# A causal convolution on one core: the middle outputs are finished by an accumulating DMA instead of VectorE

## The chip, the core and the metric

The kernel runs on one core of a Trainium2 chip. The core has five engines that matter here. TensorE (PE in the profile, with PEld for its weight loads) multiplies matrices into PSUM. VectorE (DVE) and ScalarE (ACT) do elementwise work on SBUF and PSUM. GpSimd (POOL) and SyncE (SP) issue DMAs here; POOL also makes a tiny copy now and then. Each engine runs its own list of instructions in the order in which it was written, and waits on semaphores where data of another engine or of a DMA is needed. The DMAs of all engines are carried by the same 16 DMA engines, those of SP through queue q1 and those of POOL through queue q0.

The metric is the device time of one execution in microseconds.

## The reference

```python
def reference(x, kernel):          # x: 8 x 4096 x 512, kernel: 8 x 512 x 512, f32
    out = np.zeros_like(x)
    for k in range(8):
        shifted = x if k == 0 else np.concatenate(
            [np.zeros((B, k, D)), x[:, :-k, :]], axis=1)
        out += np.matmul(shifted, kernel[k])
    return out
```

It is a causal convolution along the sequence with eight taps, and each tap is a 512 x 512 matrix. Output row t is the sum over k of x[t - k] times kernel[k].

## The kernel before

**Layout.** The 8 x 4096 rows of x are cut into 128 runs of 256 rows; run number is the partition. One "row" of the kernel is therefore 128 x 512 values, and a matmul takes 128 x 128 of it against a 128 x 512 piece of a weight. Four such matmuls are a *product* (`product`, L115 to L119): one row of 512 against one 512 x 512 matrix.

**Algorithm.** After four head rows that are computed directly, each block of 12 output rows is made with a nested Karatsuba-like scheme. The outer level splits a block into four *nodes*, PL, MI, H1 and H0, each of which is a smaller convolution of 4 output rows with combined inputs (sums and differences of rows, made on VectorE as Z, S, A and F) and combined weights. There are 21 blocks and so 84 nodes. For PL, MI and H1 a node has nine products of four matmuls, 36 matmuls; H0 is a leaf with eleven products, 44.

**What a node's result becomes.** Each node leaves two PSUM tiles, `p[LO]` and `p[HI]`, of two rows each. Step `e0` finishes the LO tile, step `e1` the HI tile (`node_e`, L225 to L244). With b for LO or HI:

- PL: ScalarE writes cc[b] = 0.5 PL (L229).
- MI: VectorE writes dd[b] = cc[b] - 0.5 MI, in a new tile (L232).
- H1: VectorE writes y = H1 + dd[b], stored as the first four rows of the block.
- H0: VectorE writes dd[b] = dd[b] - H0 in place, stored as the last four rows.
- `middle` (L246 to L249; steps `g0` for LO and `g1` for HI): VectorE writes cc[b] = 2 cc[b] - dd[b], which is half of PL + MI, and stores it as the middle four rows.

The tiles cc, dd and y come from one pool of five buffers (`y_tile`, L222). A tile is taken over when the last reader of the buffer's earlier tile is done, a DMA's landing included. All stores but one go through SP (`store`, L217).

**Order.** It is written out by hand. The first block is a long list of single steps (L506 to L594); from node 5 on the table SLOT gives each kind of node its steps:

```python
    SLOT = {
        PL: "s l00 F1 a0 l01 u l11 e0 s0 z s1 v0 F0 A x dt d0 v1 d1 l10 a1 e1",
        MI: "s l01 l00 F1 a0 u l11 e0 s0 z s1 dt A F0 v0 x v1 d1 l10 d0 e1 a1",
        H1: "s l00 F1 a0 l01 u l11 s0 dt e0 z s1 A F0 g0 v0 d0 r v1 d1 l10 e1",
        H0: "s l00 F1 b1 l01 a0 u e0 l11 s0 z s1 dt F0 A v0 x d0 g1 v1 d1 l10 a1 e1",
    }
```

Steps l00 to l11, a0, a1, b1, u, v0 and v1 are products on TensorE. Steps s, z, A, F0 and F1 make the inputs on VectorE, d0 and d1 are VectorE steps on PSUM. Steps s0, s1 and dt are ScalarE's: s0 and s1 (`node_seed`, L183) copy a partial result of the next node into its PSUM tiles, and the matmuls of v0 and later add to it. Much of a node's input work is done one or two nodes ahead: in step names "cur" is the node of the slot, s, s0, F0, v0, a0 and u belong to the next one, and z, A and a1 to the one after it.

**DMAs for the input.** Step `r` of H1 (`rows_ahead`) lets POOL make a small copy that waits for VectorE's A (`behind`, L106), and then issue three loads of x for a later block (L87; cast to bf16, into DRAM scratch xd). Step x lets SP issue the transposing DMAs from xd to the ring buffer XR (L94), two in PL and one in MI. So the order on POOL is: copy, three loads, and again in the next block. In blocks 19 to 21 nothing is left to load. In the first block the step r of H1 is written after g1 of H0, not before it.

Of the kernel before, what the change touches and what calls it, by code (L numbers as in the profile page):

```python
# [14 lines left out]
def kernel(  # L15
# [6 lines left out]
    nc = tc.nc  # L22
# [11 lines left out]
    ADD = mybir.AluOpType.add  # L34
    SUB = mybir.AluOpType.subtract
    MUL = mybir.AluOpType.mult
# [3 lines left out]
    orr = out.rearrange("b (g t) d -> (b g) t d", t=RUN)  # L40
# [39 lines left out]
    def tt(o, a, b, op):  # L80
        nc.vector.tensor_tensor(out=o, in0=a, in1=b, op=op)  # L81
# [135 lines left out]
    def store(t, y):  # L217
        nc.sync.dma_start(out=orr[:, t:t + 2, :], in_=y)

    cc, dd = {}, {}  # L220

    def y_tile():  # L222
        return ypool.tile([P, 2, D], f32, name="y")

    def node_e(n, b_):  # L225
        p, t = n.p[b_], n.t + 2 * b_
        if n.a == PL:
            cc[b_] = y_tile()
            nc.scalar.mul(out=cc[b_], in_=p, mul=0.5)  # L229
        elif n.a == MI:  # L230
            dd[b_] = y_tile()
            nc.vector.scalar_tensor_tensor(out=dd[b_], in0=p, scalar=-0.5,  # L232
                                           in1=cc[b_], op0=MUL, op1=ADD)
        elif n.a == H1:
            y = y_tile()
            tt(y, p, dd[b_], ADD)
            store(t, y)
        elif n.k == len(nodes) - 1 and b_ == HI:
            for j, eng in enumerate((nc.scalar, nc.sync)):
                tt(dd[b_][:, j], dd[b_][:, j], p[:, j], SUB)  # L240
                eng.dma_start(out=orr[:, t + 8 + j, :], in_=dd[b_][:, j])
        else:
            tt(dd[b_], dd[b_], p, SUB)
            store(t + 8, dd[b_])  # L244

    def middle(n, b_):  # L246
        nc.vector.scalar_tensor_tensor(out=cc[b_], in0=cc[b_], scalar=2.0,  # L247
                                       in1=dd[b_], op0=MUL, op1=SUB)
        store(n.t + 4 + 2 * b_, cc[b_])  # L249

    def load_w(tap):
        n = K - 1 - tap
# [85 lines left out]
    def step(k):  # L338
# [11 lines left out]
        def rows_ahead():  # L350
# [14 lines left out]
            "v0": (nxt, lambda: node_v(nxt, 0)), "v1": (nxt, lambda: node_v(nxt, 1)),  # L365
            "d0": (nxt, lambda: node_d(nxt, 0)), "d1": (nxt, lambda: node_d(nxt, 1)),
            "e0": (cur, lambda: node_e(cur, 0)), "e1": (cur, lambda: node_e(cur, 1)),
            "x": (cur, moves), "r": (cur, rows_ahead), "g0": (cur, lambda: middle(cur, 0)), "g1": (cur, lambda: middle(cur, 1)),
        }
        return acts  # L370
# [258 lines left out]
```

## Time and profile before

| | |
|---|---|
| median of 2 runs (lowest to highest) | 746.35 us (746.24 to 746.46) |
| span of the profiled execution, first to last instruction | 744.5 us |
| TensorE busy | 729.4 us, 98% |
| VectorE busy | 694.6 us, 93% |
| ScalarE busy | 241.3 us, 32% |
| POOL busy | 57.4 us, 8% |
| L247 on VectorE (the middle outputs) | 42 instructions, 51.1 us |
| L229 on ScalarE (0.5 PL) | 42 instructions, 43.1 us |
| q1 (SP) / q0 (POOL), share of the 16 DMA engines | 49.5% / 28.0% |
| read / written in HBM | 77.33 MB / 99.09 MB |
| granted TensorE clock | 1.00 |

In the page, the span goes from the first to the last instruction of the profiled execution; the runs' times also hold what lies around it, 1.9 us here. The median stands for runs without the details. A line such as "L87 POOL ... xd<-in_x_dram x3" means: code line 87, engine POOL, writes xd, reads in_x_dram, three instructions. In timelines the first column is the start and the second the duration, both in us. Busy shares are averages over the span and don't by themselves say which engine sets the end.

### The profile page before, as it was taken

Reading aid. Unit: us, or ns where it says so; the run is one execution under the profiler, and the core shown is the slowest. Engines: PE = TensorE matmul, PEld = TensorE weight load, DVE = VectorE, ACT = ScalarE, POOL = GpSimd, SP = SyncE. Lnnn points to the kernel's source line nnn. Section 1 sums busy time; section 2 is a strip of 40 time slices with the busy share of each in tenths; the row PEclk is TensorE's granted clock in tenths of the full one; section 3 lists DMA queues with packets and bytes.
Section 4 is the critical chain, followed back from the end, with each engine's and each line's share of the span. In section 5 each row is a group of like instructions: output and inputs, shape, how many; then the busy total and the mean of one; then the engine's idle time right before and its main releaser. Section 6 shows DMA issues by size and latency. Waiting matters only on the chain.

```text
span 744.5 us, 8887 instructions
## 1 busy us (share of the span) xinstructions
PE 729.4 (98%) x3362; PEld 331.6 (45%) x3430; DVE 694.6 (93%) x725; ACT 241.3 (32%) x368; POOL 57.4 (8%) x98
## 2 busy tenths in 40 slices
PE   8989999999999999999999999999999999999997
PEld 4434444444444444444444444444444444444443
DVE  1989999999999999999999999999999999999996
ACT  3053333332333333232323323242333323333331
POOL 4200010101010010101011010101101010100000
PEclk9999999999999999999999999999999999999999
DMA  9994979696886969697795969678595968865314
GB/s 202 210 208 134 227 152 246 138 237 160 199 208 160 247 136 241 148 219 185 183 233 136 246 141 234 170 178 238 138 242 137 248 156 189 220 148 194 124 78 170
DMA packets 159371, 138.88 MB, mean 187 GB/s; under 512 B 130144, under 2 KB 134240, under 8 KB 159200
## 3 DMA queue, kind: packets, MB, share of 16 engines
q1 hardware_dynamic: 145456, 99.89, 49.5%
q0 software_dynamic: 13728, 38.15, 28.0%
q8 instruction: 27, 0.44, 0.3%
q10 hardware_dynamic: 144, 0.26, 0.1%
q14 instruction: 16, 0.13, 0.0%
HBM read 77.33 MB, written 99.09 MB: 237 GB/s over the span
## 4 chain that ended last, share of the span: by engine, by line
PE 89%; DVE 4%; issue 1%; ACT 1%; DVEq 0%; ACTq 0%
PE pp L117 89%; DVE Z L81 1%; DVE y L81 1%; DVE S L81 0%; DVE w L81 0%; DVE y L247 0%; DVE A L81 0%; DVE pp L81 0%; DVE F L81 0%; ACT pp L187 0%; ACT pp L168 0%; ACT y L229 0%; ACT pp L189 0%; DVEq L624 0%; DVEq L81 0%
## 5 line engine op out<-in xcount | busy, mean ns | idle before, releaser
L117 PE MATMUL pp<-w,S 128*128 128x512 bf16 x1175 | 274.3, 379 | 1.3
L117 PE MATMUL pp<-w,F 128*128 128x512 bf16 x970 | 244.9, 379 | 1.1
L117 PEld LDWEIGHTS <-S 128*128 128x128 bf16 x1200 | 117.1, 98 | 142.9 <-issue 3.4
L117 PE MATMUL pp<-w,A 128*128 128x512 bf16 x661 | 170.6, 379 | 2.8 <-ACT pp L189 1.2
L81 DVE TENSOR_TENSOR Z<-XR 128x2048 bf16<-128x2048 bf16 (+3 forms) x109 | 154.2, 1432 | 0.1
L117 PEld LDWEIGHTS <-F 128*128 128x128 bf16 x992 | 97.0, 98 | 117.1
L81 DVE TENSOR_TENSOR S<-Z 128x2560 bf16<-128x2560 bf16 (+1 forms) x85 | 124.3, 1464 | 0.0
L187 ACT COPY pp<-pp 128x512 f32<-128x512 f32 (+1 forms) x84 | 57.8, 688 | 154.8 <-PE pp L117 152.0
L117 PEld LDWEIGHTS <-A 128*128 128x128 bf16 x672 | 65.2, 97 | 83.2 <-DVE A L81 4.4
L171 ACT COPY pp<-pp 128x512 f32<-128x512 f32 x62 | 35.3, 570 | 197.1 <-PE pp L117 197.1
L117 PE MATMUL pp<-w,Z 128*128 128x512 bf16 x330 | 85.4, 379 | 0.3
L81 DVE TENSOR_TENSOR F<-S 128x1024 bf16<-128x1024 bf16 x124 | 84.5, 682 | 0.0
L106 POOL COPY junk<-A 128x2 bf16<-128x2 bf16 x18 | 17.6, 977 | 557.6 <-DVE A L81 557.6
L189 ACT ACTIVATE pp<-pp 128x512 f32<-128x512 f32 (+1 forms) x84 | 58.6, 698 | 5.4 <-DVE y L232 2.8
L232 DVE SCALAR_TENSOR_TENSOR y<-pp,y 128x1024 f32<-128x1024 f32 x42 | 51.3, 1220 | 9.4 <-PE pp L117 9.0
L81 DVE TENSOR_TENSOR A<-Z 128x1024 bf16<-128x1024 bf16 x84 | 57.7, 686 | 1.4
L229 ACT ACTIVATE y<-pp 128x1024 f32<-128x1024 f32 x42 | 43.1, 1027 | 42.1 <-PE pp L117 40.1
L206 DVE SCALAR_TENSOR_TENSOR pp<-pp,DT 128x512 f32<-128x512 f32 x62 | 42.9, 692 | 14.3 <-PE pp L117 13.6
L81 DVE TENSOR_TENSOR y<-pp,y 128x1024 f32<-128x1024 f32 x42 | 51.1, 1216 | 1.8 <-DMA out_dram<-y 1.6
L81 DVE TENSOR_TENSOR y<-y,pp 128x1024 f32<-128x1024 f32 (+1 forms) x43 | 50.9, 1185 | 2.0 <-PE pp L117 2.0
L247 DVE SCALAR_TENSOR_TENSOR y<-y 128x1024 f32<-128x1024 f32 x42 | 51.1, 1216 | 0.0
L117 PEld LDWEIGHTS <-Z 128*128 128x128 bf16 x336 | 32.8, 98 | 39.7 <-DVE w L81 0.3
(28 smaller groups left out, 241.3 us busy)
## 6 DMA issues: line engine op xcount, KB each, us to landing
out_dram<-y SPq DMA_DIRECT2D x127, 512.0 KB, 7.5
xd<-in_x_dram POOLq DMA_DIRECT2D x61, 512.0 KB, 10.8
w<-in_kernel_dram POOLq DMA_DIRECT2D x8, 512.0 KB, 15.8
w<-in_x_dram SPq DMA_DIRECT2D x1, 1024.0 KB, 4.8
w<-in_x_dram POOLq DMA_DIRECT2D x2, 512.0 KB, 13.5
XR<-xd SPq DMA_TRANSPOSE x61, 5.0
w<-in_x_dram POOLq DMA_DIRECT2D x2, 256.0 KB, 18.5
w<-in_x_dram POOLq DMA_DIRECT2D x1, 384.0 KB, 20.1
```

The lines of the kernel that those rows point to most:

```text
L81: nc.vector.tensor_tensor(out=o, in0=a, in1=b, op=op)
L106: nc.gpsimd.tensor_copy(out=junk, in_=z[:, 0:2])
L117: nc.tensor.matmul(bank, lhsT=comp[:, c * P:(c + 1) * P], rhs=w[:, c, :], start=start and c == 0, stop=c == DC - 1, skip_group_check=True)
L171: nc.scalar.copy(out=n.q[:, 0], in_=n.q[:, 1])
L187: nc.scalar.copy(out=o, in_=q)
L189: nc.scalar.mul(out=o, in_=q, mul=-1.0)
L206: nc.vector.scalar_tensor_tensor(out=p[:, 0], in0=p[:, 1], scalar=-1.0, in1=DT, op0=MUL, op1=SUB)
L229: nc.scalar.mul(out=cc[b_], in_=p, mul=0.5)
L232: nc.vector.scalar_tensor_tensor(out=dd[b_], in0=p, scalar=-0.5, in1=cc[b_], op0=MUL, op1=ADD)
L247: nc.vector.scalar_tensor_tensor(out=cc[b_], in0=cc[b_], scalar=2.0, in1=dd[b_], op0=MUL, op1=SUB)
```

## The change

PL is now stored as it is: ScalarE copies it from PSUM to cc[b], which goes to the middle rows of the output at once, and ScalarE writes a second tile, dd[b] = -0.5 PL. MI adds half of itself to dd[b] in place, so dd[b] now holds the negative of what it held. H1 subtracts dd[b] instead of adding it; H0 writes -dd[b] - H0. `middle` is no longer a VectorE instruction and a store: POOL issues a DMA that adds dd[b] to the middle rows that are already in DRAM, so that PL becomes PL - 0.5 PL + 0.5 MI. Steps g0 and g1 keep their places in the written order.

```diff
         if n.a == PL:
             cc[b_] = y_tile()
-            nc.scalar.mul(out=cc[b_], in_=p, mul=0.5)
+            nc.scalar.copy(out=cc[b_], in_=p)
+            store(t + 4, cc[b_])
+            dd[b_] = y_tile()
+            nc.scalar.mul(out=dd[b_], in_=p, mul=-0.5)
         elif n.a == MI:
-            dd[b_] = y_tile()
-            nc.vector.scalar_tensor_tensor(out=dd[b_], in0=p, scalar=-0.5,
-                                           in1=cc[b_], op0=MUL, op1=ADD)
+            nc.vector.scalar_tensor_tensor(out=dd[b_], in0=p, scalar=0.5,
+                                           in1=dd[b_], op0=MUL, op1=ADD)
         elif n.a == H1:
             y = y_tile()
-            tt(y, p, dd[b_], ADD)
+            tt(y, p, dd[b_], SUB)
             store(t, y)
         elif n.k == len(nodes) - 1 and b_ == HI:
             for j, eng in enumerate((nc.scalar, nc.sync)):
-                tt(dd[b_][:, j], dd[b_][:, j], p[:, j], SUB)
+                nc.vector.scalar_tensor_tensor(out=dd[b_][:, j], in0=dd[b_][:, j], scalar=-1.0,
+                                               in1=p[:, j], op0=MUL, op1=SUB)
                 eng.dma_start(out=orr[:, t + 8 + j, :], in_=dd[b_][:, j])
         else:
-            tt(dd[b_], dd[b_], p, SUB)
+            nc.vector.scalar_tensor_tensor(out=dd[b_], in0=dd[b_], scalar=-1.0,
+                                           in1=p, op0=MUL, op1=SUB)
             store(t + 8, dd[b_])

     def middle(n, b_):
-        nc.vector.scalar_tensor_tensor(out=cc[b_], in0=cc[b_], scalar=2.0,
-                                       in1=dd[b_], op0=MUL, op1=SUB)
-        store(n.t + 4 + 2 * b_, cc[b_])
+        nc.gpsimd.dma_start(out=orr[:, n.t + 4 + 2 * b_:n.t + 6 + 2 * b_, :], in_=dd[b_], accum_op=ADD)
```

## The prediction

> **What bounds the kernel now.** I read the page's busy shares first, then the chain that ended last, then the group of the removed instruction.
>
> ```profile
> PE 729.4 (98%) x3362; PEld 331.6 (45%) x3430; DVE 694.6 (93%) x725; ACT 241.3 (32%) x368; POOL 57.4 (8%) x98
> PE 89%; DVE 4%; issue 1%; ACT 1%; DVEq 0%; ACTq 0%
> L247 DVE SCALAR_TENSOR_TENSOR y<-y 128x1024 f32<-128x1024 f32 x42 | 51.1, 1216 | 0.0
> ```
>
> TensorE (PE) is busy for 98% of the span and makes 89% of the chain; from 600 us on the chain is 95% matmuls. In a steady block of four nodes, 402.5 to 435.4 us, 152 weight loads go by in 32.9 us, 0.216 us each: TensorE never pauses. So the 51.1 us that leave VectorE can come back only where TensorE waits for it, and the list of waits has 4.4 us of that (19 waits of weight loads for VectorE's A, 0.2 us each). That is the ceiling of the gain. The loss has no ceiling: whatever stops TensorE is added to the end.
>
> **The place that decides.** The second accumulate of a block (step g1 of the H0 node) reads dd[1], and e1 of the same node overwrites dd[1]. In before, L247 and e1 follow each other on VectorE. After, e1 must wait until a DMA has finished. So I read the timeline where g1 and e1 stand (start, duration, engine, line), with the three loads that POOL issues ahead of g1.
>
> ```profile
> 406.40 1.53 POOL L87 DMA_DIRECT2D xd<-in_x_dram  x3
> ...
> 413.81 1.22 DVE L247 SCALAR_TENSOR_TENSOR y<-y 128x1024 f32<-128x1024 f32 x1
> ...
> 415.55 1.21 DVE L81 TENSOR_TENSOR y<-y,pp 128x1024 f32<-128x1024 f32 x1
> ...
> 416.68 1.48 DVE L81 TENSOR_TENSOR S<-Z 128x2560 bf16<-128x2560 bf16 x1
> ...
> 418.08 0.68 DVE L81 TENSOR_TENSOR F<-S 128x1024 bf16<-128x1024 bf16 x1
> ...
> 418.36 1.03 PE L117 MATMUL pp<-w,Z 128*128 128x512 bf16 x4
> 418.56 1.02 ACT L229 ACTIVATE y<-pp 128x1024 f32<-128x1024 f32 x1 [1.98 <-PE pp L117]
> ...
> 419.22 1.03 PE L117 MATMUL pp<-w,F 128*128 128x512 bf16 x4
> 419.48 0.59 ACT L187 COPY pp<-pp 128x512 f32<-128x512 f32 x1
> ...
> 420.12 1.67 PE L117 MATMUL pp<-w,S 128*128 128x512 bf16 x7
> ```
>
> To be seen: e1 (415.55) is followed on VectorE by S and then F (F1 of the next node), which ends at 418.76; product l11 at 419.22 reads that F. TensorE has nothing else to do after u (418.36): its program is in order.
>
> When would g1 land? POOL's own wait is for A (L106), then it issues three loads in 1.53 us, then g1, whose data was ready long before. The answers on DMA, for L87 in this block and for the queues from 400 to 420 us:
>
> ```profile
> L87 POOL DMA_DIRECT2D xd<-in_x_dram x3: 515/515/515, 406.4 to 407.4; - x3
> DMA to landing us min/median/max: 7.3/10.6/13.9
> ...
> q0 software_dynamic: 421, 1.56, 42.1%
> q1 hardware_dynamic: 569, 2.11, 29.9%
> ```
>
> Three loads issued 0.5 us apart land 3.8 us apart: POOL's one queue (q0) works them off one after the other, and a fourth transfer stands behind them. The third lands at 407.4 + 13.9 = 421.3. In 20 us q0 took 8.4 us of all 16 engines for 3 loads, 2.8 us a load; q1 took 6.0 us for 2.11 MB, four stores, 1.5 us a store.
>
> **The parts, and their sum.**
>
> 1. VectorE loses 42 L247 (51.1 us). Value taken: nothing on the path, bounds 0 and a gain of 4.4 us. The A that weight loads wait for is made ahead of g0, so even the 4.4 us mostly stay; and the time ahead of e1 becomes waiting, since e1 needs l10, which ends near 414.9.
>
> 2. g1 behind loads. In the window three stores share the engines with the loads (those issued at 406.4, 407.6 and 410.1); the first is g0's and goes (those of 415.1 and 416.8 stand in q1 behind them), so the third load lands about 1.5 us earlier, at 419.8. An accumulate is in no row of the trace. Its bounds: a store's 1.5 us (same bytes out of SBUF) and twice a load's, 5.6 us. I take a load's 2.8 us, the nearest row: 1 MB read for 512 KB written, as here from two sources, on the same queue. g1 lands at 422.6, where e1 could run at 415.1 (l10 done). From the start of e1 to the end of F1 is 3.2 us, and 0.25 us pass from weight load to matmul: l11 starts at 422.6 + 3.45 = 426.05 in place of 419.22. TensorE stands still for 6.9 us. Behind e1 on VectorE stand S, F1, z and all the rest, so nothing goes around it. With the bounds: 5.6 to 9.7 us.
> How often: POOL's copy L106 runs 18 times, once for each group of three loads. In the first block the written order puts g1 ahead of that group; in the last three there is no group. So 17 of 21 blocks pay: 17 x 6.9 = 117 us (95 to 165).
>
> 3. Restart of TensorE. The only start from standstill in the trace is the first:
>
> ```profile
> 1.20 4.83 PE L282 MATMUL pp<-DT 128*128 128x512 bf16 x14 [1.20 <-DVE DT L378]
> ```
>
> 14 matmuls in 4.83 us, where 14 x 0.216 is 3.0: 1.8 us lost, although the clock row says 1.00 there. After the 0.91 us pause at 11.09 us nothing is lost (20 matmuls in 4.48 us). A pause of 6.9 us is unlike the second; I take 1.8 us, 17 x 1.8 = 31 us (bounds 0 and 31).
> The Trainium skill, "TensorE: Matmul & The Clock Gate", section "Why this matters for your kernels", says that gaps above about 3 us between matmul bursts send the array back to half clock. It speaks against the change; by its 3.4 us window at half clock an estimate would be 1.7 us a gap, 29 us in all. The start-up row fits it, the granted clock shown there does not.
>
> 4. ScalarE. At PL the one L229 (1.03 us) becomes a copy (L187's wide form, 1.00) and a multiply (1.03): 42 us more, 241 to 283 us, cheap for an engine at 32%, but not everywhere. In e0 of PL it stands directly ahead of seeds s0 and s1: L187 follows L229 at 419.48, and the matmuls on its result start at 420.12, while l11 ends near 420.25. One more us there delays v0 by about 0.95 us. In the 17 blocks behind a stalled e1 this is hidden: e0 waits for l00 and l01 only, so ScalarE does both passes while TensorE stands still for F1. Four PL nodes have no such cover (the first, and those behind the four free blocks, less the last block, which has no successor): 4 x 0.95 = 4 us. Were there no stall anywhere, it would be 21 x 0.95 = 20 us. In e1 of PL the next ScalarE work still finds 1.94 us of idle time (427.28), which covers it.
>
> 5. g0 (step of H1) is issued once MI's e0 has made dd[0], near 426.7, with q0 empty, and is due at H0's e0 near 441.7: 15 us for a transfer whose kind lands in 4 to 7 us when alone. Nothing; what is late if that cover goes is in the rivals.
>
> 6. The queues. SP keeps 127 stores: 42 move from behind L247 to behind ScalarE's copy, ahead of the transposes of PL (first issue 420.72, after e0's copy at 419.6). POOL gets 42 issues of 0.52 us, 22 us against 557.6 us of waiting. The rings get 42 x 2.8 = 118 us on about 78% of 744 us. In the first block loads 28 to 36 move behind g0, from about 35 us to 66 us; their transposes are issued at 91.8. Nothing.
>
> 7. Signs: e0/e1 of MI keep their form, those of H1 a TENSOR_TENSOR (1.22), those of H0 change to a SCALAR_TENSOR_TENSOR (1.22 for 1.21). Six y tiles on five buffers stay; the 1.6 us wait for a buffer at the end goes, off the path. Nothing.
>
> Sum: 744.5 + 117 + 31 + 4 = 896.5 us of span. The runs' median lies 1.9 us above the span, so **898 us**.
>
> **Rivals.**
>
> A. q0 does not make g1 wait for the loads. For: it is issued at 408, and a first load lands after 7.3 us; then it is there at about 415.5 to 416 and e1 loses under 1 us. Against: the loads' landings in order. It leaves ScalarE's pass, 20 us, and at most 1 us in 17 blocks: 766 to 785.
>
> B. Not slower: the accumulate is done before e1, and s0 is not delayed. It decides at two points: g1 landed by 415.6, and s0 done by 420.25. Then only the 4.4 us of waits can go: 742 to 746. Against: before l11 ends there is only about 0.2 us of room for a 1.0 us pass.
>
> C. More than forecast: the accumulates also hold H0's e0, or POOL holds the loads back behind g0 until a store has landed, 1 to 4 us a block on top of 2's upper bound: 946 to 1015.
>
> That the removed work stays is no rival: the diff deletes L247 and puts nothing on VectorE in its place.
>
> **How the numbers follow.** Chances: forecast 0.79, A 0.09, B 0.05, C 0.07. The forecast's own bounds are 744.5 + 95 + 0 + 4 + 1.9 = 845 and 744.5 + 165 + 31 + 4 + 1.9 = 946. At the low end the third load could come another 1.5 us earlier if the two stores left cost the loads less (17 x 1.5 = 26: 819); at the high end C's first us (17: 963). Range 819 to 963, which leaves out A, B and most of C. Measurement of this kernel tells about 2% from no change (761 us). Forecast, A and C are above it, 0.95; B is within it but for a small chance of a larger gain: faster 0.01, same 0.05, slower 0.94.
>
> **What would show it.** Right: VectorE's wait at the changed H0 line for a DMA out_dram<-y, 17 times some 7 us; after each, matmuls at less than full pace for some us; VectorE's busy time 51 us lower, ScalarE's 42 higher; the last three blocks at about 33 us. Wrong: no such wait (A, B); waits at e0 as well (C); a fourth q0 transfer that lands with the loads.

## The result and the profile after

The changed kernel takes 890.14 us (median of 2 runs, 888.75 to 891.54) against 746.35 us before: 1.193 times as long, 95% interval 1.188 to 1.197. The profiled execution has a span of 887.0 us against 744.5, so 142.5 us have to be found.

The page of the changed kernel: busy time by engine, the rows of TensorE, its granted clock and the DMAs in 40 slices, and the chain by engine.

```profile
PE 770.3 (87%) x3430; PEld 338.7 (38%) x3430; DVE 657.2 (74%) x683; ACT 281.3 (32%) x410; POOL 83.0 (9%) x140
PE   8989979797979797887979797978879797979997
PEclk9999999898989898989989898989898898989999
DMA  9969986777777787777677787877677777786926
PE 38%; DMA 28%; DVE 21%; issue 4%; POOL 3%; ACT 1%; DVEq 0%; SPq 0%; POOLq 0%; ACTq 0%
```

VectorE is 37 us less busy in the page (not 51: instructions that follow each other at once overlap by some 0.08 us in the records, which is counted once, and fewer do so now), and TensorE's share fell from 98% to 87%. The chain that was 89% TensorE now runs through a DMA for 28% of the span and through VectorE for 21%. TensorE's clock, full throughout before, dips in nearly every second slice of the middle. The DMA row, with slices of 22 us, is mostly at 70 to 80%. It can't tell whether the wait comes from one transfer's place or from a lack of bandwidth; the stretches further down and the experiments can.

The list of waits names it (who waits, for whom: total us, times, longest):

```profile
DVE y L246 <- DMA out_dram<-y: 134.8, 17, 8.7
PE pp L117 <- DVE F L81: 100.3, 17, 6.7
PE pp L117 <- ACT pp L187: 4.0, 4, 1.7
```

Line 246 is what e0 and e1 of H0 have become. It waits 17 times for a DMA on the output, TensorE waits 17 times for VectorE's F behind it, and 4 times for ScalarE's seed. One block in the timeline (start, duration, engine, line), with the copy and the three loads on POOL, g1 (L251) behind them, and e1:

```profile
441.37 0.19 POOL L106 COPY junk<-A 128x2 bf16<-128x2 bf16 x1 [10.35 <-DVE A L81]
441.85 1.60 POOL L87 DMA_DIRECT2D xd<-in_x_dram  x3 [0.29 <-issue]
443.43 0.94 POOL L251 DMA_DIRECT2D out_dram<-y  x1
...
454.38 1.03 PE L117 MATMUL pp<-w,Z 128*128 128x512 bf16 x4
...
457.78 1.22 DVE L246 SCALAR_TENSOR_TENSOR y<-y,pp 128x1024 f32<-128x1024 f32 x1 [7.69 <-DMA out_dram<-y]
458.92 1.49 DVE L81 TENSOR_TENSOR S<-Z 128x2560 bf16<-128x2560 bf16 x1
...
460.32 0.69 DVE L81 TENSOR_TENSOR F<-S 128x1024 bf16<-128x1024 bf16 x1
...
461.06 1.89 PE L117 MATMUL pp<-w,F 128*128 128x512 bf16 x4 [5.66 <-DVE F L81]
...
462.74 3.08 PE L117 MATMUL pp<-w,S 128*128 128x512 bf16 x8
...
465.66 1.03 PE L117 MATMUL pp<-w,F 128*128 128x512 bf16 x4
```

The landing times in this block, of the three loads and of the one accumulate, each from its own issue:

```profile
DMA to landing us min/median/max: 6.1/9.4/12.3
...
DMA to landing us min/median/max: 14.3/14.3/14.3
```

The third load, issued at 442.9, lands at 455.2; g1, issued at 443.43, lands at 457.7, and e1 starts at once. Beside the loads SP now has two stores (issued at 442.40 and 445.51) where there were three. TensorE ends u near 455.4 and has nothing until F is there.

The matmuls after the pause are slow: the twelve from 461.06 to 465.66 take 4.60 us, 0.38 each, where twelve at 0.216 take 2.59. The stretches before, in and after the pause show the clock (length; busy time of PE, PEld, DVE, ACT and POOL; then granted clock, DMA share, GB/s):

```profile
440.00:455.20 15.20, 15.20 (x72) 6.73 (x70) 9.46 (x10) 3.43 (x7) 2.71 (x5) 1.00 0.88 206
455.20:461.00 5.80, 0.20 (x1) 0.00 (x0) 3.22 (x4) 2.89 (x5) 0.00 (x0) 0.77 0.49 138
461.00:465.30 4.30, 4.24 (x11) 1.56 (x12) 3.68 (x5) 0.00 (x0) 0.00 (x0) 0.52 0.51 165
465.30:480.70 15.40, 15.40 (x73) 6.97 (x72) 13.49 (x16) 6.44 (x9) 0.87 (x1) 1.00 0.81 177
```

While the loads run, the DMA engines are 88% busy, in the pause 49%. The clock falls to half during the pause and stays there for about 4 us of work: the matmuls start 0.43 us apart up to 464.88, and 0.216 us from 465.23 on. The clock records in the trace show such a dip in each of the 17 pauses. It begins 2.8 to 3.6 us after the last matmul and is 6.83 us long; 4.1 us of it, on the mean, lie behind the pause, and half of that, 2.06 us, is work lost.

**The account.** POOL's copies L106, one a block, are 40.93 us apart on the mean (113.68 to 768.60, 16 blocks) against 32.89 before (109.35 to 635.58): 8.04 us a block. 17 x 8.04 = 136.7. The four waits for ScalarE's seed are 4.0 us, but 0.7 us of them (in the first block) were there before, so 3.3 are new; together 140.0 of 142.5 us. The 2.5 us left are in the first two blocks, most of them in the second, where VectorE waits 1.1 us for a late transpose; the experiments come back to that.

### The profile page after: what moved, and what is told of

Same layout as the page of the kernel before. It is cut to its first block, busy times and chain, and to the rows that moved or that the text cites. A ratio compares the mean times of both kernels' runs of the same rounds, so it can differ in the third digit from the quotient of the medians.

```text
span 887.0 us, 9061 instructions
## 1 busy us (share of the span) xinstructions
PE 770.3 (87%) x3430; PEld 338.7 (38%) x3430; DVE 657.2 (74%) x683; ACT 281.3 (32%) x410; POOL 83.0 (9%) x140
## 4 chain that ended last, share of the span: by engine, by line
PE 38%; DMA 28%; DVE 21%; issue 4%; POOL 3%; ACT 1%; DVEq 0%; SPq 0%; POOLq 0%; ACTq 0%
PE pp L117 38%; DMA out_dram<-y 28%; DVE S L81 5%; DVE Z L81 4%; POOL xd L87 3%; DVE y L246 2%; DVE y L234 2%; DVE y L81 2%; DVE F L81 2%; DVE A L81 1%; DMA XR<-xd 1%; ACT y L232 1%; DVE pp L81 0%; POOL junk L106 0%; DVE w L81 0%
## 5 line engine op out<-in xcount | busy, mean ns | idle before, releaser
L117 PE MATMUL pp<-w,F 128*128 128x512 bf16 x992 | 262.0, 396 | 100.3 <-DVE F L81 100.3
L117 PE MATMUL pp<-w,S 128*128 128x512 bf16 x1200 | 296.8, 399 | 2.5 <-ACT pp L187 2.4
L117 PEld LDWEIGHTS <-S 128*128 128x128 bf16 x1200 | 123.6, 103 | 164.9 <-issue 38.3
L246 DVE SCALAR_TENSOR_TENSOR y<-y,pp 128x1024 f32<-128x1024 f32 x41 | 50.1, 1221 | 147.9 <-DMA out_dram<-y 134.8
L187 ACT COPY pp<-pp 128x512 f32<-128x512 f32 (+1 forms) x84 | 57.4, 683 | 183.9 <-PE pp L117 136.0
L251 POOL DMA_DIRECT2D out_dram<-y x42 | 37.9, 901 | 586.5 <-DVE y L234 561.9
L189 ACT ACTIVATE pp<-pp 128x512 f32<-128x512 f32 (+1 forms) x84 | 58.8, 701 | 4.3 <-DVE y L234 2.8
L229 ACT COPY y<-pp 128x1024 f32<-128x1024 f32 x42 | 42.7, 1016 | 42.1 <-PE pp L117 42.1
L81 DVE TENSOR_TENSOR pp<-DT,pp 128x512 f32<-128x512 f32 x62 | 42.9, 692 | 16.3 <-PE pp L117 16.3
```

Of the source, the lines that this page charges most:

```text
L117: nc.tensor.matmul(bank, lhsT=comp[:, c * P:(c + 1) * P], rhs=w[:, c, :], start=start and c == 0, stop=c == DC - 1, skip_group_check=True)
L187: nc.scalar.copy(out=o, in_=q)
L189: nc.scalar.mul(out=o, in_=q, mul=-1.0)
L229: nc.scalar.copy(out=cc[b_], in_=p)
L246: nc.vector.scalar_tensor_tensor(out=dd[b_], in0=dd[b_], scalar=-1.0, in1=p, op0=MUL, op1=SUB)
L251: nc.gpsimd.dma_start(out=orr[:, n.t + 4 + 2 * b_:n.t + 6 + 2 * b_, :], in_=dd[b_], accum_op=ADD)
```

## The experiments

The theory: e1 waits until g1 has read dd[HI], and g1 is late because it stands behind three loads in POOL's queue; each pause of TensorE costs its own length, and then half of the time that the clock stays at half; ScalarE's second pass is hidden behind the pause, and costs up to 20 us where there is none. Rivals: the accumulate is slow in itself; the added traffic is what costs; the slow matmuls after the pause have another cause. All edits but the control's are to the changed kernel. Ratios are to the kernel before as it ran beside each experiment (medians 746.35 to 747.31 us).

### g1 ahead of the loads

```diff
-        H1: "s l00 F1 a0 l01 u l11 s0 dt e0 z s1 A F0 g0 v0 d0 r v1 d1 l10 e1",
-        H0: "s l00 F1 b1 l01 a0 u e0 l11 s0 z s1 dt F0 A v0 x d0 g1 v1 d1 l10 a1 e1",
+        H1: "s l00 F1 a0 l01 u l11 s0 dt e0 z s1 A F0 g0 v0 d0 v1 d1 l10 e1",
+        H0: "s l00 F1 b1 l01 a0 u e0 l11 s0 z s1 dt F0 A v0 x d0 g1 r v1 d1 l10 a1 e1",
```

(Step r finds its rows and its A from the next node in place of the one after it, so POOL does the same copy and loads for the same block.)

> Edit: the written order puts g1 ahead of the three loads on POOL (step r moves from H1 to H0, behind g1); all else as in the changed kernel. Theory (g1 lands late because it stands behind three loads in q0): VectorE's wait at e1 for a DMA, 134.8 us in 17 times, goes; the clock stays at 1.00; what is left is ScalarE's second pass ahead of s0, 21 x 0.95 = 20 us: 746.35 + 20 = 766 us (762 to 770). Rival 1 (the accumulate by itself, or the load on the 16 DMA engines, makes it late): the waits stay, 860 us or more. Rival 2 (ScalarE's pass costs nothing): 742 to 748 us.

Measured: 767.01 us, 1.027 times the kernel before (1.0253 to 1.0288). The clock is at 1.00. No wait of VectorE for an accumulate is left. In this kernel an accumulate lands 5.5 to 6.4 us after its issue (the 18 between 380 and 700 us; 5.0 to 7.2 in all blocks from the second on), and g1 is issued as soon as MI's e1 is done. So neither the accumulate's own time nor its traffic makes the 143 us by itself; its place in the queue does. What is left is one wait, in this kernel's list of TensorE's waits:

```profile
PE pp L117 <- ACT pp L187: 17.5, 21, 1.7
```

One in each of the 21 PL nodes, 0.79 us in a steady block, which is 0.91 us longer than before (33.80 against 32.89): ScalarE's second pass, now that no pause hides it. That it is this pass, the late multiply below tests.

### Another tile for e1's result

```diff
+            y = cc[b_] if b_ == HI else dd[b_]
-            nc.vector.scalar_tensor_tensor(out=dd[b_], in0=dd[b_], scalar=-1.0,
+            nc.vector.scalar_tensor_tensor(out=y, in0=dd[b_], scalar=-1.0,
                                            in1=p, op0=MUL, op1=SUB)
-            store(t + 8, dd[b_])
+            store(t + 8, y)
```

> Edit: H0's e1 writes its result to the tile cc[HI], whose store has long landed, and not over dd[HI]; g1 stays behind the loads, no DMA is moved. Theory (the loss is the wait of e1 for g1's read of dd[HI]): no wait at e1, g1 still lands 14 us after its issue, and the time is that of the kernel with g1 ahead of the loads: 766 us (762 to 770). Rival 1 (the extra DMA traffic itself slows TensorE or the loads): over 800 us.

Measured: 768.07 us, 1.028 (1.0265 to 1.0296). All DMAs keep their order, g1 still stands behind the loads (14.1 to 16.5 us from issue to landing), and the loss is about the same 20 us. The first experiment took the lateness away, this one takes away the one who waits for it; either is enough. The traffic rival falls.

### Zero matmuls in the pause

```diff
+    def idle_work(n):
+        for _ in range(20):
+            nc.tensor.matmul(n.q[:, 1], lhsT=nil, rhs=W[n.a, MID, MID][:, 0, :],
+                             start=False, stop=True, skip_group_check=True)
-        PL: "s l00 F1 a0 l01 u l11 e0 s0 z s1 v0 F0 A x dt d0 v1 d1 l10 a1 e1",
+        PL: "s l00 F1 a0 l01 u i l11 e0 s0 z s1 v0 F0 A x dt d0 v1 d1 l10 a1 e1",
```

(`nil` is a tile of zeros; step i is made in the 17 blocks that wait.)

> Edit: in the 17 blocks that wait, TensorE gets 20 matmuls with a weight of zeros (4.3 us, adding zero to a bank in use) between u and l11, inside the 5.8 us in which it stands still. Theory (2.0 us of each block are matmuls at half clock after the pause): the matmuls after l11's start are 0.216 us apart from the first, the granted clock stays near 1.00, and 17 x 2.0 = 34 us go: 856 us (850 to 862). Rival (the slow matmuls after the pause come from late inputs or from VectorE, not from the clock): 885 to 895 us.

Measured: 863.95 us; mean clock 0.993 against 0.933. 340 matmuls more, and 26 us less. TensorE in one block of this kernel:

```profile
443.49 4.48 PE L186 MATMUL pp<-w,nil 128*128 128x512 bf16 x20
449.18 1.04 PE L118 MATMUL pp<-w,F 128*128 128x512 bf16 x4 [1.21 <-DVE F L82]
450.06 1.89 PE L118 MATMUL pp<-w,S 128*128 128x512 bf16 x8
```

After the rest of the pause the first four matmuls take 1.04 us, where they took 1.89, and the next eight 1.89 in place of 3.08. The inputs and VectorE's work are the same, so the slow matmuls were the clock. Of the 34 us 8 are missing: the mean rest of the pause is 29.8 / 17 = 1.75 us and goes up to 2.9, the pause with its zeros is about 0.2 us a block longer than before (1.75 + 4.32 against 5.90), 17 x 0.17 = 3 us; and in two of the 17 blocks the clock fell all the same, behind rests of 2.1 and 2.9 us, which by the clock records costs 1.7 and 3.0 us.

### Two loads ahead, one behind

```diff
+        def last_rows():
+            if nxt and nxt.t + 2 * STEP < RUN:
+                load_x(nxt.t + 3 * STEP - 4)
-                for t in range(two.t + 2 * STEP, two.t + 3 * STEP, 4):
+                for t in range(two.t + 2 * STEP, two.t + 3 * STEP - 4 * late, 4):
-        H0: "... x d0 g1 v1 d1 l10 a1 e1",
+        H0: "... x d0 g1 r2 v1 d1 l10 a1 e1",
```

(`late` is 1 but in the first block; r2 calls `last_rows`.)

> Edit: from the second block on only two of the three loads are issued ahead of g1, the third behind it. Theory: the second load lands 10.0 us after the first one's issue, g1 2.5 us later, where e1 could run at about 9.3 us: TensorE stands still for about 2.6 us in place of 5.8. By the clock theory a pause that short might keep the clock: 890 - 17 x (3.2 + 2.0) = 802 us, with 17 x 2.0 more (836 us) if it doesn't. Rival (the accumulate is late whatever stands ahead of it): 885 to 895 us.

Measured: 845.32 us, between the two kernels, as the queue theory wants: the loss goes with what stands ahead. The size was missed. TensorE's waits for F are 60.4 us in 17 times, 3.6 each and not 2.6: in the block looked at g1 lands 13.8 us after the first load's issue and not 12.5, and the load issued behind it only 2.4 us later, so the two seem to have shared the engines; that reading was not tested. And most pauses of this length already cost the clock: a block is 5.45 us longer (copies 38.34 us apart against 32.89), 1.9 of it after the pause. The length alone does not decide. Two of the 17 pauses, of 3.29 us (ending at 130.68) and of 3.11 us (ending at 474.15), each with the stretch behind it, in the columns of the stretches above:

```profile
127.30:130.70 3.40, 0.11 (x2) 0.02 (x2) 3.30 (x4) 2.78 (x5) 0.00 (x0) 1.00 0.88 252
130.70:135.00 4.30, 4.30 (x20) 1.95 (x21) 4.30 (x6) 0.00 (x0) 0.00 (x0) 1.00 0.55 178
471.00:474.10 3.10, 0.04 (x1) 0.00 (x0) 3.10 (x4) 2.73 (x5) 0.00 (x0) 1.00 0.89 256
474.10:478.50 4.40, 4.35 (x13) 1.65 (x14) 3.83 (x4) 0.00 (x0) 0.00 (x0) 0.61 0.51 160
```

Behind the longer pause TensorE runs at full pace, behind the shorter one mostly at half. The longer one is the only one of the 17 without a dip in the clock records.

### A plain copy for the accumulate

```diff
-        nc.gpsimd.dma_start(out=orr[...], in_=dd[b_], accum_op=ADD)
+        nc.gpsimd.dma_start(out=orr[...], in_=dd[b_])
```

> Edit: the changed kernel with POOL's DMA of g0 and g1 as a plain copy, no addition (left out: the middle rows then hold only the negated mean). Theory (an accumulate costs a load's time in the queue, since it reads two sources): g1 lands 1.0 us nearer to the third load than the 2.5 us of the accumulate, 17 x 1.0 = 17 us less: 873 us (866 to 878). Rival 1 (an accumulate costs what a store does): 886 to 894 us. Rival 2 (the accumulate is the main cost): below 800 us.

Measured: 868.43 us (two runs, 865.4 and 871.5). VectorE's waits are 115.7 us in place of 134.8. In the 17 blocks that wait g1 lands 1.2 us behind the third load (1.21 to 1.25), with the addition 2.5 us (median; 2.3 to 3.4); over all 42, the median landing is 4.0 us against 6.2. On POOL an issue takes 0.55 us against 0.9. So in the queue an accumulate costs about twice a plain store, and the addition itself is some 22 of the 144 us, within a few us, as the two runs lie 6 us apart. Most of the rest is the wait behind the loads, with the clock that it costs.

### The late multiply

```diff
-            dd[b_] = y_tile()
-            nc.scalar.mul(out=dd[b_], in_=p, mul=-0.5)
+            if b_ == HI:
+                minus(b_)
+    def minus(b_):
+        dd[b_] = y_tile()
+        nc.scalar.mul(out=dd[b_], in_=cc[b_], mul=-0.5)
-        PL: "s l00 F1 a0 l01 u l11 e0 s0 z s1 v0 F0 A x dt d0 v1 d1 l10 a1 e1",
+        PL: "s l00 F1 a0 l01 u l11 e0 s0 z s1 v0 F0 A x dt n0 d0 v1 d1 l10 a1 e1",
```

(on top of g1 ahead of the loads; n0 calls `minus(LO)`)

> Edit: g1 ahead of the loads, and in PL's e0 ScalarE's multiply for dd[LO] is moved behind step dt (it reads cc[LO] in place of PSUM). Theory (what is left of the loss there is the 1.03 us pass ahead of s0): TensorE's waits for L187, 17.5 us in 21 times, go but for the first; 746.35 us less at most 4.4 us of waits for A: 742 to 748 us. Rival (the 20 us left come from something else, the DMAs or the store of PL): 760 us or more.

Measured: 748.89 us, 1.0026 (1.0015 to 1.0036), 1 us above the range. The 18 us were ScalarE's pass; TensorE's waits for L187 are down to 1.0 us in 2 times. The same on top of the other tile:

> Edit: e1 of H0 writes to cc[HI], g1 stays behind the loads, and the multiply for dd[LO] stands behind dt. Theory: as with g1 ahead of the loads, 742 to 748 us; that g1 lands 14 us after its issue costs nothing where nobody waits for it. Rival (late accumulates or their traffic cost something of their own): 5 us or more above the kernel with g1 ahead of the loads.

Measured: 749.83 us, 1.0032 (1.0023 to 1.0041), 2 us above the range. The runs of the two overlap, so late accumulates that nobody waits for cost at most about 1 us. Both lie 2 to 3 us above the kernel before, where 1 was the most expected.

### The control

> Edit: the kernel before, with step r moved behind g1 as in the first experiment and nothing else. Control: in it g1 is VectorE's work, and POOL's queue holds only the copy and the loads. Both theories: 746 us within 2.

Measured: 747.31 us, 1.0000 (0.9991 to 1.0009). The order of the loads by itself does nothing.

### Level, and a try for more

The 2 us that the late multiply leaves are in the second block, which is 35.9 us long (copies at 76.30 and 112.23) against 33.1 before; from there on the blocks are as long as before. In the first block the loads of rows 28 to 36 had moved behind g0, from about 35 us to 67.9. Writing g0 behind them there:

```diff
-    go(3, "g0")
...
     load_x(36)
+    go(3, "g0")
```

> Edit: as with g1 first and the late multiply, and in the first block g0 is written behind the loads of rows 28 to 36, so that they are issued as early as in the kernel before. Theory (of the 2 us that this kernel still lies above the one before, all is in the second block, where transposes that came late make A 1.1 us late, and TensorE is 2.8 us longer): 2 to 3 us less, 746 to 747 us, level with the kernel before. Rival (the 2 us come from ScalarE's multiply elsewhere): 748 to 750 us.

Measured: 746.73 us, 1.0009 (1.0000 to 1.0018): level with the kernel before. Every part of the loss has been taken away by an edit of its own, and with 40 us less on VectorE than before (654 against 695 us in the late-multiply kernel) the time is the same: TensorE is the bound. The last try uses VectorE's free time to make A earlier:

```diff
-        H1: "s l00 F1 a0 l01 u l11 s0 dt e0 z s1 A F0 g0 v0 d0 v1 d1 l10 e1",
+        H1: "s l00 F1 a0 l01 u l11 s0 dt z A e0 s1 F0 g0 v0 d0 v1 d1 l10 e1",
```

> Edit: the last one, and in H1 VectorE's z and A stand ahead of e0, for which VectorE has time now. Theory: the 19 waits of weight loads for A (0.2 us each, 5 us in all) go: 742 to 743 us. Rival (the freed VectorE time can't be turned into TensorE time, since seeds or products are late in its place): 746 us or more.

Measured: 765.26 us, 1.0253 (1.0239 to 1.0267). The weight loads' waits for A are gone, and others have come, in this kernel's list:

```profile
PE pp L117 <- ACT pp L189: 16.4, 20, 1.2
ACT pp L189 <- DVE y L81: 41.4, 20, 2.3
```

Seed s1 (L189) needs the bank that e0 has to read first, and e0 is now late: 20 waits of ScalarE for VectorE's y, then 20 of TensorE for the seed. No version beat the kernel before.

## Why the prediction was right, point by point

The forecast was 898 us with 152 us of loss in the span; measured were 890 us and 142.5. The mechanism held, and some sizes were off in opposite directions: 17 us too much for the pauses, 5 too little for the restarts, and 2.5 us in the first blocks that were put at nothing.

| term of the sum | forecast | measured |
|---|---|---|
| blocks that wait | 17 | 17 |
| third load lands after the first one's issue | 13.4 us | 13.35 us |
| accumulate behind it | 2.8 us | 2.5 us |
| TensorE stands still, each | 6.9 us | 5.9 us (100.3 / 17) |
| restart at half clock, each | 1.8 us | 2.1 us (8.04 - 5.9) |
| ScalarE ahead of s0 | 4 us in 4 nodes | 4.0 us in 4, of them 3.3 new |
| first two blocks, what is left | nothing | 2.5 us |

1. *VectorE's 51 us come back as nothing:* shown. With all the new waits removed the kernel takes 746.7 us. Even the 4.4 us of waits for A stayed, as the step said. VectorE's busy time was to fall by 51 us and fell by 37, for the reason given with the page.

2. *g1 behind the loads, e1 behind g1:* shown from both sides, by moving g1 and by moving e1's result. The pause was set 1 us too long. About half of that is POOL's copy ahead of the loads: before, the loads came 0.98 us after the copy's start, now 0.48, because VectorE no longer runs L247 beside it (see below). I had taken the loads' issue time from before without asking what would change just ahead of it. 0.3 us are the accumulate and 0.1 the way from g1's landing to l11.

3. *Restart of TensorE:* the mechanism is shown by the zero matmuls and by the clock rows; 2.1 us where the first start of the trace had given 1.8. One reading of the prediction was wrong: it set the clock row's 1.00 at the start against the slow matmuls there. The clock records of that trace begin only at 4.55 us, and the row shows 1.00 where there is no record. The first eight matmuls start 0.43 us apart, from 4.57 us on it is 0.216: the start is at half clock too, and (4.55 - 1.20) / 2 = 1.7 us are lost there. That 1.8 came so near to 2.1 is in part luck, since by the clock records the cost differs from pause to pause, 1.6 to 2.5 us, with the moment at which TensorE starts again within the dip. The Trainium skill's page "TensorE: Matmul & The Clock Gate" ("Why this matters for your kernels") warned of gaps above about 3 us, and the runs agree roughly. All pauses of 5.4 to 6.7 us cost the clock, and so did 16 of the 17 of 3.1 to 4.6 us, 1.9 us each on the mean; of the 17 rests of 1.2 to 2.9 us in the kernel with zeros two did. No single length divides them.

4. *ScalarE:* shown. Hidden 17 times, 4.0 us in the 4 nodes without cover. Without the stall 20 us were worked out, and the span with g1 first is 20.1 us longer (764.6 against 744.5): 17.5 us are TensorE's waits, 0.8 us each, while a steady block is 0.91 us longer where 0.95 was taken.

5. *g0 costs nothing:* right in steady blocks.

6. *The queues:* "nothing" was wrong by about 2 us. In the first block the three loads that went behind g0 made transposes late in the second; putting them back took 1.5 of the 1.9 us by which the span of the late-multiply kernel lies above that of before (746.4 and 744.9 us against 744.5).

7. *Signs and tiles:* nothing, as forecast; the level version contains them all.

Of the rivals, A (g1 not held up by the loads, 766 to 785) is what the kernel with g1 first does, 767.0; it fell because in POOL's queue g1 landed behind the third load in all 17 blocks. C fell as well: VectorE's 17 waits for a DMA are those of e1, and there is none at e0.

## What to carry to other kernels

When an engine's work is turned into a DMA, its place in the written order no longer says when it is done: look at what stands ahead of it in its queue and at who next writes over its source. Give the small transfer that somebody waits for its place ahead of bulk loads that nobody waits for yet, or let the next writer use another tile. In this kernel, with TensorE 98% busy, taking 40 us from VectorE was worth nothing, and nearly every pause of more than 3 us cost about 2 us on top for the clock.

## What the runs showed of the hardware

POOL's copy of 128 x 2 values (L106) takes 1.05 us before and 0.19 us after. In before, VectorE runs L247 beside it, from 405.20 to 406.42, and the copy, started at 405.42, ends at 406.46, just after L247. In the block at 307 us the copy starts later in L247, at 307.05, takes 0.68 us, and again ends with it. In the first block of before, where VectorE reads PSUM beside it, the copy takes 0.18 us; in the control, where L247 is back beside it, 1.05 in all but two. The Trainium skill, "SBUF — State Buffer", section "Who interferes with whom", says that a VectorE instruction with two SBUF inputs contends with a GpSimd instruction that reads SBUF. L247 has two, the PSUM form one, and the traces agree.

The profile's granted clock is 0.52 where twelve matmuls behind a pause take 0.38 us each, eleven gaps mostly of 0.43 us and then of 0.216. At the start of a trace, ahead of the first clock record, the 1.00 in that row means nothing: the gaps between matmuls show the clock there.

A 512 KB accumulate from SBUF into DRAM with nothing ahead of it lands 5.5 to 6.4 us after its issue; as the last of four in the queue it lands 2.5 us behind the load ahead of it, a plain copy 1.2 us.
